# Moving the attention's maxima steps within each run of six score tiles

## The chip, the core and the metric

The kernel runs on one core of a Trainium2 chip. The metric is the device time of one execution in microseconds; the time before is the median of three runs. TensorE (PE) multiplies matrices and writes its results to PSUM, VectorE (DVE), ScalarE (ACT) and GpSimd (POOL) do the rest, SyncE (SP) issues most transfers.

## The reference

One layer of a hybrid block over 2048 latent tokens and 256 context tokens, width 1024, all in fp32. Cut to what matters here:

```python
k_all = jnp.concatenate([k_c, k_x], axis=2)        # 256 context + 2048 latent keys, 2 key heads
v_all = jnp.concatenate([v_c, v_x], axis=2)
s = jnp.einsum('bkgqd,bknd->bkgqn', q, k, preferred_element_type=jnp.float32)
p = jax.nn.softmax(s, axis=-1).astype(v.dtype)     # 8 query heads of 64, 2048 queries
o = jnp.einsum('bkgqn,bknd->bkgqd', p, v)
```

Ahead of it stand a modulated norm and one wide input projection, behind it the merge with a gated branch, an output projection and a squared-ReLU MLP with a residual.

## The kernel before

The program is one straight list of instructions in stages: input projection, attention, merge, MLP. The attention (`attend`) works through 16 units, each a block of 512 queries times a pair of query heads. A unit has 18 key tiles of 128 keys, taken in three runs (groups) of six.

For each key tile, `Unit.scores(j)` takes two PSUM banks (one for each head of the pair) and makes 8 matmuls, four for each head; the two heads use the two halves of the array's rows, so the matmuls run in pairs (line 1780). ScalarE then turns each bank into exponentials (line 1790) and gives it back. The matmuls contract over 64 rows: products of split high and low parts, and one that subtracts the query's reference value, a maximum over its scores.

That maximum is found ahead of time, for later units, by `Unit.maxima(n)`, which does n steps of a list `todo`. A step takes two PSUM banks, makes two matmuls of 512 columns (or four of 256 for the context keys; line 1736) from the high parts alone, and VectorE reduces each bank to a column of maxima (lines 1747 and 1742). A unit has 18 steps: two for the context, 16 for the latent keys. In the first two runs of a unit the steps belong to the next unit (`nxt`), in the third run to the one behind it (`far`); each run does six steps, as long as there is such a unit. When a unit's 18 steps are done, `reference` takes the maximum over them on VectorE (lines 1753 and 1754), and `low_queries` turns the result with four transposes on TensorE (line 186) at the end of the third run.

The values of a run (`Unit.values`, line 1800) are multiplied one run later: `pend` keeps them, and they follow the next run's scores. `values(0)` takes the output's PSUM bank, `leave` copies it out and gives it back (line 1830). Sums of exponentials are built on POOL (line 1823) and for four key tiles on VectorE (line 1820); `join` adds the two, `sums` adds over the partitions on TensorE (line 1842), copied by ScalarE (line 1848).

All score, maxima, transpose and output tiles of the attention share one tag of eight PSUM banks, `self.psum({"b": 8})`. Which bank a tile gets, and so which semaphore its first matmul waits on, is settled when the program is built. The order of work is the order in which `attend` issues it: `fixed` holds TensorE and VectorE to that order, and `order` adds dependencies so that tiles of one tag are first written in the order in which they were made.

Of the kernel before, what the change touches and what calls it, by code (L numbers as in the profile page):

```python
# [70 lines left out]
class Kern:  # L71
# [748 lines left out]
    def attend(self, units, late):  # L820
        begin = self.here()
        pend, self.ready = [], []
        for i, u in enumerate(units):
            at = lambda n: units[n] if 0 <= n < len(units) else None
            nxt, far, old, older = at(i + 1), at(i + 2), at(i - 1), at(i - 2)
            for gi, g in enumerate(range(0, NKT, GROUP)):
                group = range(g, g + GROUP)
                step = nxt if gi < 2 else far
                if not nxt and gi == 0:
                    raws = [self.br_raw(m, self.t2) for m in range(2)]  # L830
                for j in group:
                    u.scores(j)
                    if step:
                        step.maxima(1)
                    if gi == 0 and j == 2 and far:
                        far.load()
                if gi == 2 and nxt:
                    nxt.low_queries()
                if gi == 2 and i in FIRST_INPUTS:
                    next(late, None)  # L840
                for f in pend:
                    f()
                if gi == 1 and far:
                    far.queries()
                if gi == 0 and far:
                    far.cast()
                if gi == 2 and old:
                    old.sums()
                if gi == 0:
                    if older:  # L850
                        older.inverse()
                    if far:
                        far.remainder()
                if gi == 1:
                    if nxt:
                        nxt.reference()
                    if old:
                        old.join()
                if gi == 2 and i in FIRST_INPUTS:
                    next(late, None)  # L860
                if not nxt and gi:
                    self.ready.append(self.br_weights(raws.pop(0), self.t2))
                pend = [lambda u=u, j=j: u.values(j) for j in group]
            pend.append(u.leave)
        for f in pend:
            f()
        units[-2].inverse()
        self.fixed.append(range(begin, self.here()))
# [1039 lines left out]
```

## Time and profile before

| what | us |
|---|---|
| median of three runs (2993.07 to 2994.03) | 2993.59 |
| the profiled execution | 2993.09 |
| its span, first to last instruction | 2991.3 |
| TensorE busy | 2965.5 |
| VectorE busy | 2023.0 |
| ScalarE busy | 1355.5 |

The granted TensorE clock is 0.999 in the mean. The attention's scores run from 757.6 to 1384.1 us of the span. In the rows of a timeline the first number is the start in us from the span's start, the second the length of the merged rows, then engine, line, operation, output and inputs, tile, element types and the count; in brackets stands how long the engine was idle before and what it waited for. In the rows of waits stand the total in us, how often, and the longest.

### The profile page before, as it was taken

What the parts mean: (1) busy time and instruction counts of PE and PEld (TensorE: products, weight loads), DVE (VectorE), ACT (ScalarE), POOL (GpSimd) and SP (SyncE); (2) the same over time, 40 slices, a digit from 0 to 9 for tenths busy, and PEclk for the clock granted to TensorE, in tenths of its full rate; (3) what the DMA queues carried; (4) which work ended last, traced back from release to release, by engine and by line L of the source; (5) the groups of instructions that cost most, each with busy time, mean ns of one, the idle gap of its engine ahead of it and who ended that gap; (6) DMA issues with size and microseconds to landing.
All of it is one profiled execution on the core that took longest, in us unless ns stands there. A gap on an engine that the chain in (4) does not pass through costs nothing.

```text
span 2991.3 us, 39857 instructions
## 1 busy us (share of the span) xinstructions
PE 2965.5 (99%) x14973; PEld 2301.8 (77%) x14973; DVE 2023.0 (68%) x2999; ACT 1355.5 (45%) x2058; POOL 564.9 (19%) x420
## 2 busy tenths in 40 slices
PE   7999999999999999999999999999999999999999
PEld 5888888887656565655888888888888888888887
DVE  6848567585777778886655698786656766654455
ACT  4443434342555555554322264444554344444433
POOL 0000000000788999990000000000000000000000
PEclk9999999999999999999999999999999999999999
DMA  7464646643100000012766558898676544446665
GB/s 240 121 220 122 222 141 196 181 133 109 36 12 16 12 22 20 25 33 97 242 177 183 154 186 314 310 327 305 225 241 227 183 155 155 155 149 219 208 216 204
DMA packets 330275, 485.53 MB, mean 162 GB/s; under 512 B 28953, under 2 KB 161345, under 8 KB 330082
## 3 DMA queue, kind: packets, MB, share of 16 engines
q1 hardware_dynamic: 326242, 478.40, 48.3%
q10 hardware_dynamic: 3840, 4.59, 0.4%
q8 instruction: 117, 1.92, 0.3%
q14 instruction: 76, 0.62, 0.1%
HBM read 348.56 MB, written 134.35 MB: 161 GB/s over the span
## 4 chain that ended last, share of the span: by engine, by line
PE 97%; DVE 2%; DMA 1%; SPq 0%; issue 0%; ACT 0%; ACTq 0%; DVEq 0%
PE b L1362 13%; PE b L1361 13%; PE b L1360 13%; PE b L180 11%; PE b L182 11%; PE b L181 11%; PE b L1780 9%; PE b L1800 8%; PE b L1736 2%; PE b L186 2%; DMA w<-in_w_mod 1%; PE b L1842 0%; PE b L290 0%; DVE ts L1747 0%; DVE ac L1820 0%; DVE f L1490 0%
## 5 line engine op out<-in xcount | busy, mean ns | idle before, releaser
L1467 DVE TENSOR_TENSOR f<-f,f 128x1024 fp32r<-128x1024 f32 x224 | 264.7, 1222 | 257.1 <-ACT f L1466 254.6
L1747 DVE TENSOR_REDUCE ts<-b 128x1 f32<-128x512 f32 x512 | 311.6, 682 | 105.8 <-PE b L1736 105.8
L1360 PE MATMUL b<-f,f 128*128 128x512 f32 x896 | 349.3, 390 | 0.0
L1361 PE MATMUL b<-f,f 128*128 128x512 f32 x896 | 349.0, 390 | 0.0
L1362 PE MATMUL b<-f,f 128*128 128x512 f32 x896 | 348.7, 389 | 0.0
L1466 ACT CAST f<-f 128x1024 fp32r<-128x1024 f32 x224 | 224.6, 1052 | 263.6 <-PE b L1361 255.4
L1780 PE MATMUL b<-t,t 64*128 64x512 f32 x2304 | 330.9, 400 | 0.0
L1780 PEld LDWEIGHTS b<-t,t 64*128 64x128 f32 x2304 | 226.2, 184 | 69.3 <-issue 26.0
L1823 POOL TENSOR_TENSOR ac<-ac,p 128x512 f32<-128x512 f32 x204 | 269.0, 1353 | 43.4 <-ACT p L1790 43.4
L1823 POOL TENSOR_TENSOR ac<-ac,t 128x512 f32<-128x512 f32 x146 | 233.1, 1626 | 0.0
L1790 ACT ACTIVATE p<-b 128x512 f32<-128x512 f32 x384 | 206.7, 598 | 48.3 <-PE b L1780 41.5
L152 DVE TENSOR_TENSOR w<-w,w 128x1024 fp32r<-128x1024 f32 x120 | 146.8, 1223 | 114.4 <-ACT w L148 76.3
L180 PE MATMUL b<-t,w 128*128 128x512 f32 x512 | 203.2, 397 | 0.4 <-DVE ts L1742 0.3
L182 PE MATMUL b<-t,w 128*128 128x512 f32 x512 | 199.7, 390 | 0.0
L181 PE MATMUL b<-t,w 128*128 128x512 f32 x512 | 199.5, 390 | 0.0
L1361 PEld LDWEIGHTS b<-f,f 128*128 128x128 f32 x896 | 168.2, 188 | 35.9 <-DVE f L1467 1.6
L1360 PEld LDWEIGHTS b<-f,f 128*128 128x128 f32 x896 | 168.2, 188 | 34.8
L1362 PEld LDWEIGHTS b<-f,f 128*128 128x128 f32 x896 | 168.2, 188 | 34.8
L180 PE MATMUL b<-w,t 128*128 128x512 f32 (+1 forms) x528 | 191.5, 363 | 0.2 <-DVE t L150 0.2
L148 ACT CAST w<-w 128x1024 fp32r<-128x1024 f32 x120 | 126.0, 1050 | 145.0 <-DMA w<-in_w_in 108.9
L182 PE MATMUL b<-w,t 128*128 128x512 f32 (+1 forms) x528 | 190.5, 361 | 0.1
L181 PE MATMUL b<-w,t 128*128 128x512 f32 (+1 forms) x528 | 190.1, 360 | 0.0
(261 smaller groups left out, 6120.8 us busy)
## 6 DMA issues: line engine op xcount, KB each, us to landing
w<-in_w_in SPq DMA_DIRECT2D x120, 512.0 KB
ao_d<-f SPq DMA_DIRECT2D x224, 256.0 KB
f<-ao_d SPq DMA_DIRECT2D x112, 512.0 KB
f<-w2o_d SPq DMA_DIRECT2D x112, 512.0 KB
f<-in_w_ff SPq DMA_DIRECT2D x48, 1024.0 KB
w2o_d<-f SPq DMA_DIRECT2D x112, 256.0 KB
md<-in_w_mod SPq DMA_DIRECT2D x32, 512.0 KB
f<-x_d SPq DMA_DIRECT2D x64, 256.0 KB
```

Source lines behind the costliest of these rows:

```text
L180: mm(ps, sh, mh, start=start, stop=False, skip_group_check=skip)
L181: mm(ps, sh, ml, start=False, stop=False, skip_group_check=skip)
L182: mm(ps, sl, mh, start=False, stop=stop, skip_group_check=skip)
L1360: mm(ps, wh, hh, start=start and k == 0, stop=False, skip_group_check=True)
L1361: mm(ps, wh, hl, start=False, stop=False, skip_group_check=True)
L1362: mm(ps, wl, hh, start=False, stop=k == len(w) - 1, skip_group_check=True)
L1466: self.nc.scalar.copy(h, f32(l))
L1467: self.nc.vector.tensor_tensor(out=l, in0=f32(l), in1=f32(h), op=ALU.subtract)
L1747: nc.vector.tensor_reduce(out=self.mx[:, t, h, c : c + 1], in_=ps[h], axis=AX.X, op=ALU.max)
L1780: self.nc.tensor.matmul(ps[h], keys[h], q[rows[h]], start=n == 0, stop=n == len(steps) - 1, skip_group_check=True,)
L1800: nc.tensor.matmul(self.o[h * HD : (h + 1) * HD, :], k.V[c][:, i, self.kv * HD : (self.kv + 1) * HD], pt[h], start=j == 0, stop=j == NKT - 1,)
L1823: nc.gpsimd.tensor_tensor(out=self.acc[e][:, h], in0=old[:, h], in1=pt[h], op=ALU.add)
```

## The change

In each run of six key tiles one maxima step followed the scores of each tile. Now none follows the first tile, one follows each of the next four, and two follow the last. Each run still does six steps in the same order.

```diff
                 for j in group:
                     u.scores(j)
-                    if step:
-                        step.maxima(1)
+                    if step and j > g:
+                        step.maxima(1 if j < group[-1] else 2)
                     if gi == 0 and j == 2 and far:
                         far.load()
```

## Prediction

> **What bounds the kernel now.** I read the page first, for the busiest engine and the chain that ends last, and then the timeline of each engine over one stretch of the attention.
>
> ```profile
> span 2991.3 us, 39857 instructions
> PE 2965.5 (99%) x14973; PEld 2301.8 (77%) x14973; DVE 2023.0 (68%) x2999; ACT 1355.5 (45%) x2058; POOL 564.9 (19%) x420
> PE 97%; DVE 2%; DMA 1%; SPq 0%; issue 0%; ACT 0%; ACTq 0%; DVEq 0%
> ```
>
> TensorE (PE) is busy for 99% of the span and carries 97% of the chain that ended last. An edit that neither adds nor removes work can therefore only change how tightly TensorE is packed. The groups of the attention's window give the count of the moved work, and the chain shows what a run of six key tiles costs when no maxima stand in it (the last unit):
>
> ```profile
> L1736 PE MATMUL b<-t,t 64*128 64x512 f32 (+1 forms) x584 | 120.6, 368 | 0.3 <-DVE ts L1747 0.2
> 1356.45 5.68 PE b L1780 x48
> 1367.43 5.71 PE b L1780 x48
> ```
>
> The 584 matmuls are 28 context steps of four and 236 of two: 264 steps, 44 runs of six. One run of TensorE, the third of a unit (L1780 a score set, L1736 a maxima step):
>
> ```profile
> 899.93 1.20 PE L1780 MATMUL b<-t,t 64*128 64x512 f32 x8
> 900.96 0.40 PE L1736 MATMUL b<-t,t 64*128 64x256 f32 x4
> 901.20 1.08 PE L1780 MATMUL b<-t,t 64*128 64x512 f32 x8
> 902.12 0.40 PE L1736 MATMUL b<-t,t 64*128 64x256 f32 x4
> 902.36 1.20 PE L1780 MATMUL b<-t,t 64*128 64x512 f32 x8
> 903.40 0.39 PE L1736 MATMUL b<-t,t 64*128 64x512 f32 x2
> 903.63 1.07 PE L1780 MATMUL b<-t,t 64*128 64x512 f32 x8
> 904.53 0.39 PE L1736 MATMUL b<-t,t 64*128 64x512 f32 x2
> 904.76 1.16 PE L1780 MATMUL b<-t,t 64*128 64x512 f32 x8
> 905.76 0.39 PE L1736 MATMUL b<-t,t 64*128 64x512 f32 x2
> 905.99 1.14 PE L1780 MATMUL b<-t,t 64*128 64x512 f32 x8
> 906.96 0.40 PE L1736 MATMUL b<-t,t 64*128 64x512 f32 x2
> 907.29 0.65 PE L186 MATMUL b<-ident,t 128*128 128x128 f32 x4
> ```
>
> I call the score sets S0 to S5 and read each one's end as the start of the row behind it. A free set takes 0.91 (901.20 to 902.12, 903.63 to 904.53), the first of a run 1.03, a maxima step 0.24, the last step until the next stage 0.33. Nothing waiting, a run would be 1.03 + 5 x 0.91 + 5 x 0.24 + 0.33 = 7.11 us; it is 7.36. So 0.25 is lost to waits, and they have a rhythm: the ends of S1, S3, S5 stand at 902.12, 904.53, 906.96, that is 2.41 and 2.43 apart, where free work of two tiles is 2.30. The waits and ScalarE (ACT), whose exponentials give the score banks back, say why:
>
> ```profile
> PEld b L1780 <- ACT p L1790: 10.9, 50, 0.4
> PEld b L1736 <- DVE ts L1747: 1.6, 5, 0.6
> 901.22 2.19 ACT L1790 ACTIVATE p<-b 128x512 f32<-128x512 f32 x4 [0.55 <-PE b L1780]
> 903.59 2.29 ACT L1790 ACTIVATE p<-b 128x512 f32<-128x512 f32 x4 [0.19 <-PE b L1780]
> 905.96 2.29 ACT L1790 ACTIVATE t<-b 128x512 f32<-128x512 f32 x4
> 915.42 3.25 ACT L1790 ACTIVATE p<-b 128x512 f32<-128x512 f32 x6 [0.66 <-PE b L1780]
> 918.89 1.09 ACT L1790 ACTIVATE p<-b 128x512 f32<-128x512 f32 x2 [0.22 <-PE b L1780]
> 919.98 1.09 ACT L1790 ACTIVATE t<-b 128x512 f32<-128x512 f32 x2
> ```
>
> The weight loads of score sets waited 50 times for an exponential, those of maxima five times for a reduction. There are eight PSUM banks; one holds the unit's output, and each S and each maxima step takes two of the other seven. S2 is the first to need S0's second bank. S0's pair of exponentials starts at 901.22 and takes 1.09 (the rows of two), so ends at 902.31; S2 starts at 902.36 and ends at 903.40, 1.09 behind the exponential's end. So the loop "a score set ends, its two exponentials run, the next but one set may start" turns in 2.41, not 2.30. The Trainium skill, Perfetto Trace Analysis, Optimization Strategy, says that the same gap repeated on the engine that should be full can mean too little PSUM for the next tile. By that rule the trace agrees: 0.25 in each such run.
>
> **The change, part by part.** Per run of six tiles, the first maxima step (0.24 of TensorE, two reductions of VectorE) goes from behind S0 to behind S5's own step. No instruction is added or removed; no DMA is moved: the query load of the next-but-one unit is issued by SP behind the third tile as before. Other stages keep their orders.
>
> *Front of the run.* S1 follows S0 at once: it ends at 1.03 + 0.91 = 1.94 from the run's start instead of 2.19, S2 at 1.94 + 0.24 + 0.91 = 3.09. S0, S1 and the first step fill six banks, S2 takes the seventh and S0's first, the next step takes S0's second and S1's first. S3 then needs S1's second, whoever gets the other freed ones. S0's exponentials start 1.29 into the run (901.22 less 899.93) and ScalarE needs 1.09 a tile, so S1's second ends at 1.29 + 1.09 + 1.09 = 3.47. S3 ends 1.09 later, at 4.56. Without that wait it would end at 3.09 + 0.24 + 0.91 = 4.24. So 0.32 of TensorE's lead is lost at once: before, S3 ended at 4.60 (904.53).
>
> *End of the run.* From S3 to S5 the loop turns once more: 4.56 + 2.41 = 6.97, against 7.03 before (906.96). Behind S5 there are now two steps, 0.24 + 0.33, where one of 0.33 stood: the run ends at 7.54 instead of 7.36. **Price of a third run: +0.18.** In words: S5 is paced by ScalarE through the banks and comes at the same time, 0.06 earlier, and a step that filled the pacing time ahead of it now lies behind it, where nothing waits.
>
> *First run of a unit.* Here ScalarE also has to copy the old sums first and begins later:
>
> ```profile
> 914.18 0.59 ACT L1848 COPY t<-b 128x512 f32<-128x512 f32 x1 [4.94 <-PE b L1842]
> 914.04 1.20 PE L1780 MATMUL b<-t,t 64*128 64x512 f32 x8
> 921.07 0.39 PE L1736 MATMUL b<-t,t 64*128 64x512 f32 x2
> 921.38 3.65 PE L1800 MATMUL b<-p,t 128*64 128x512 f32 x16
> ```
>
> Its exponentials start at 915.42, 1.38 into the run. S1's second ends at 3.56, S3 at 4.65, S5 at 7.06, the run at 7.06 + 0.24 + 0.31 = 7.61, against 7.34 (921.38 less 914.04): **+0.27**.
>
> *Second run of a unit.* The old output's bank is given back at its beginning and the new one is taken behind it, so eight banks turn. S3 waits for S1's second exponential if banks are handed on in the order of the tiles; only one of its two halves then waits. If they go in the order in which they come free, S3 takes one from the first maxima step and does not wait.
>
> ```profile
> 926.69 1.20 PE L1780 MATMUL b<-t,t 64*128 64x512 f32 x8
> 934.21 3.65 PE L1800 MATMUL b<-p,t 128*64 128x512 f32 x16
> 967.30 1.19 PE L1780 MATMUL b<-t,t 64*128 64x512 f32 x8
> 974.53 3.65 PE L1800 MATMUL b<-p,t 128*64 128x512 f32 x16
> ```
>
> These take 7.52 and 7.23; the floor is 7.11. Bounds: -0.12 (7.23 to the floor) and +0.18 (the third run). I take **+0.10**, nearer to the upper, since half the tile is held.
>
> *VectorE (DVE).* The first reduction comes 0.91 later and the last two end about a microsecond later.
>
> ```profile
> 901.40 2.48 DVE L1742 TENSOR_REDUCE ts<-b 128x2 f32<-128x512 f32 x4 [2.11 <-PE b L1736]
> 903.83 4.88 DVE L1747 TENSOR_REDUCE ts<-b 128x1 f32<-128x512 f32 x8
> 915.50 7.29 DVE L1747 TENSOR_REDUCE ts<-b 128x1 f32<-128x512 f32 x12 [5.24 <-PE b L1736]
> 928.14 7.37 DVE L1747 TENSOR_REDUCE ts<-b 128x1 f32<-128x512 f32 x12 [1.97 <-PE b L1736]
> ```
>
> Queued behind them are additions, the query remainder, the reference and the join, and then the next run's reductions. VectorE stood idle for 1.97 to 5.24 before each run's first reduction, and that reduction moves back by 0.91 too, so the delay is absorbed: 0. If the cover were gone, the transposes behind a third run would wait for a bank of a late reduction: a step is 4.88/4 = 1.22 of VectorE, the third run's fourth step is reduced by about 1.94 + 0.43 + 4 x 1.22 = 7.25, before the 7.54 at which they start. Upper bound 0.14 on 14 runs. *POOL and SP:* nothing is moved past either; the sums that POOL adds come from exponentials that start no later at the run's head.
>
> *Unit 0.* Its first two runs are one stretch, as no values stand between, and VectorE paces it: 24 reductions, with a remainder between. The first reduction 0.91 later bounds it at +0.91; the floor is 0, as banks freed late still gate the same last step. I take +0.2, nearer to 0, because most of its steps are gated by TensorE's own order at first.
>
> **Sum.** 14 third runs x 0.18 = 2.5, 14 first x 0.27 = 3.8, 14 second x 0.10 = 1.4, unit 0 0.2: +7.9. The profiled execution took 2993.09 (1.8 around its span), 0.5 under the median of 2993.59. 2993.1 + 7.9 = 3001.0 by that execution, 3001.5 by the median.
>
> **Rivals.** *The order is indifferent (no change, 2993.6).* Exponentials take 6 x 1.09 = 6.54 a run and reductions 7.3, both hidden over run and values together; were the banks enough, each order would run at 7.11 plus the same waits. For it: reductions hardly ever hold TensorE (1.6 in all), and small earlier ends of S5 could cancel the step behind it: at 0.24 earlier instead of 0.06 all is even. Against it: the 2.41 rhythm. The Trainium skill, Perfetto Trace Analysis, Matmuls, asks for groups that rotate through the banks so that draining one overlaps the next group's matmuls; by that rule either order is covered, and the trace agrees only in part, as a run that rotates loses 0.25.
>
> *Faster, by a busier ScalarE.* Before, ScalarE idles within a run (0.19 before 903.59, 0.22 before 918.89). With S0 and S1 together it runs through. If S3 does not have to wait for S1's second exponential, every run falls to the floor: 14 x (7.36 - 7.11) + 14 x (7.34 - 7.11) + 14 x 0.12 = 8.4, so 2985.2. It decides as soon as S3's banks are free by 3.33 - 0.15 = 3.18 of the run instead of 3.47: the 0.29 would need an eighth bank in all runs. I see that in second runs only.
>
> *Slower still.* Second runs pay 0.27 as well, unit 0 its 0.91 and third runs the 0.14 of VectorE: 2.5 + 3.8 + 3.8 + 0.9 + 2.0 = 13.0, 3006.6.
>
> **How the numbers follow.** No change can be told from a difference within 0.2%, 6.0 us. Forecast (2998 to 3004): 0.50; slower still: 0.10; indifferent: 0.28; faster: 0.12. The forecast's lower part (under 2999.6) lies within 0.2%: 0.05 of its 0.50. Hence slower 0.55, same 0.34 (0.28, 0.05, and 0.01 of the faster case, where only second runs gain), faster 0.11. The range leaves out the faster rival and nearly nothing above: 2991 to 3006.5.
>
> **What would show it.** Right: first and third runs of 7.5 to 7.6, S3's first matmul waiting on ScalarE, S5 ending near 7.0, two maxima steps back to back behind it, more waiting of L1780's loads for L1790. Wrong: runs of 7.1 to 7.3, or S3 starting at 3.33; waits of L1736 or L186 for reductions (VectorE after all); a total that moves outside of 757 to 1384 us, where no order changes.

## The result, and the profile after

| | before | after |
|---|---|---|
| median, us (22 runs each) | 2994.1 (2991.99 to 2997.19) | 2999.73 (2997.10 to 3002.41) |
| the profiled execution | 2993.09 | 2999.79 |
| its span | 2991.3 | 2998.0 |
| its attention, first to last score matmul | 626.52 | 632.02 |

The changed kernel is slower by 5.6 us: the ratio is 1.0018, 95% interval 1.0012 to 1.0024. The interval excludes a ratio of 1, so the kernel did get slower, though 5.6 is a little less than the 6.0 (0.2%) that the prediction wanted to see before it spoke of a change. The forecast was +7.9.

The page of the changed kernel's profile shows the same 14973 matmuls and the same bound; TensorE's busy time grew by 4.8 and the span by 6.7. No work was added, so the question is how the matmuls are packed.

```profile
span 2998.0 us, 39869 instructions
PE 2970.3 (99%) x14973; PEld 2293.1 (76%) x14973; DVE 2016.9 (67%) x2999; ACT 1348.8 (45%) x2058; POOL 549.5 (18%) x420
PE 97%; DVE 2%; DMA 1%; issue 0%; ACT 0%; SPq 0%; DVEq 0%; ACTq 0%
```

Where the time went is read from the length of each run, from the start of its first score matmul to the start of the stage behind it. The medians, in us, over the first and second runs of units 1 to 14 and the third runs of units 0 to 13:

| | third runs | first runs | second runs | unit 0's double run | unit 14's third run |
|---|---|---|---|---|---|
| before | 7.363 | 7.354 | 7.261 | 15.60 | 6.35 |
| after | 7.458 | 7.533 | 7.286 | 15.89 | 7.53 |
| difference of the sums | +1.21 | +2.46 | +0.38 | +0.29 | +1.18 |

(The sums are over 14 runs of a kind; unit 14's third run is apart, as no unit needs maxima there any more.) They make +5.5 of attention. The stages between the runs take 279.0 in both. The kernel outside of the attention differs by 1.2, and over all the kernels shown below it lay between 2363.8 and 2367.6, so nothing is read from that.

The third run of the changed kernel on TensorE, at the same place as the one that the prediction shows (start, length, engine, line):

```profile
901.25 2.11 PE L1780 MATMUL b<-t,t 64*128 64x512 f32 x16
...
904.66 1.21 PE L1780 MATMUL b<-t,t 64*128 64x512 f32 x8
905.71 0.40 PE L1736 MATMUL b<-t,t 64*128 64x512 f32 x2
...
907.10 1.20 PE L1780 MATMUL b<-t,t 64*128 64x512 f32 x8
908.14 0.63 PE L1736 MATMUL b<-t,t 64*128 64x512 f32 x4
908.70 0.66 PE L186 MATMUL b<-ident,t 128*128 128x128 f32 x4
```

S0 and S1 are one row of 16. S3 starts at 904.66 and ends at 905.71, 4.46 into the run; S5 ends at 908.14, 6.89; two maxima steps stand behind it, and the transposes begin at 7.45. Both S3 and S5 take 1.04 to 1.05, where a free set takes 0.91. ScalarE in that run, and the waits of the weight loads in the attention (line and what it waited for, total, times, longest):

```profile
902.54 3.10 ACT L1790 ACTIVATE p<-b 128x512 f32<-128x512 f32 x6 [0.55 <-PE b L1780]
905.97 1.08 ACT L1790 ACTIVATE p<-b 128x512 f32<-128x512 f32 x2 [0.33 <-PE b L1780]
```

```profile
PEld b L1780 <- ACT p L1790: 15.2, 48, 1.6
ACT in L148 <- DVE raw L900: 13.6, 4, 8.0
PEld b L186 <- DVE ts L1747: 4.5, 14, 0.4
PEld b L1736 <- DVE ts L1747: 1.0, 4, 0.4
```

Score sets wait longer for exponentials (15.2 us against 10.9), maxima steps no longer than before for reductions (1.0 against 1.6). A first and a second run:

```profile
915.45 2.11 PE L1780 MATMUL b<-t,t 64*128 64x512 f32 x16
...
918.95 1.21 PE L1780 MATMUL b<-t,t 64*128 64x512 f32 x8
920.00 0.40 PE L1736 MATMUL b<-t,t 64*128 64x512 f32 x2
...
922.43 0.64 PE L1736 MATMUL b<-t,t 64*128 64x512 f32 x4
923.00 1.51 PE L1800 MATMUL b<-p,t 128*64 128x512 f32 x6
```

```profile
969.15 2.14 PE L1780 MATMUL b<-t,t 64*128 64x512 f32 x16
...
972.50 1.27 PE L1780 MATMUL b<-t,t 64*128 64x512 f32 x8
...
976.44 1.08 PE L1800 MATMUL b<-p,t 128*64 128x512 f32 x4
```

In the first run S3 ends at 4.55 and S5 at 6.98, and the run at 7.55. In the second run S3 starts at 3.35, where order alone would let it start at 3.33. Only its second half waits, for S1's second exponential, which ends at 972.53 (3.38 into the run). That half stays some 0.2 behind the first: S3's row is 1.27 long, where a free one is 1.08. The lag is carried to the end of the run, at 7.29. Before had nearly the same lag: in the median of 14 second runs the last matmuls of S5's two halves start 0.18 apart before and 0.20 after.

One place was not foreseen. Unit 14's third run, the first one with no maxima, grew by as much as all third runs together. First the changed kernel's timeline there, then before's:

```profile
1347.80 3.28 PE L1780 MATMUL b<-t,t 64*128 64x512 f32 x25
1348.14 1.21 DVE L1835 TENSOR_TENSOR ac<-ac,ac 128x1024 f32<-128x1024 f32 x1
1349.28 1.78 DVE L900 TENSOR_TENSOR raw<-raw,raw 128x512 f32<-128x512 f32 x1
1351.09 0.62 ACT L148 CAST in<-raw 128x512 fp32r<-128x512 f32 x1 [8.04 <-DVE raw L900]
1351.61 4.01 ACT L1790 ACTIVATE p<-b 128x512 f32<-128x512 f32 x8
1352.26 3.14 PE L1780 MATMUL b<-t,t 64*128 64x512 f32 x23 [1.18 <-ACT p L1790]
```

```profile
1343.29 6.42 PE L1780 MATMUL b<-t,t 64*128 64x512 f32 x48
1343.60 1.78 DVE L900 TENSOR_TENSOR raw<-raw,raw 128x512 f32<-128x512 f32 x1
1345.41 0.62 ACT L148 CAST in<-raw 128x512 fp32r<-128x512 f32 x1 [6.56 <-DVE raw L900]
```

Read upward from TensorE's gap of 1.18: it waits for an exponential (L1790); ScalarE's exponentials stand in its queue behind a cast of an input of the merge (L148); the cast waits for VectorE's multiplication of that input (L900), which stands behind the join (L1835) and the late reductions of the unit's second run. The cast starts 3.29 into the run after (1351.09 less 1347.80) and 2.12 before (1345.41 less 1343.29): 1.17 later, which is the run's growth. Not all of that is the moved step: counted from the second run's start the last reduction ends 0.91 later, and the first addition behind it (L1820) takes 2.27 instead of 1.98. In the runs with maxima the next first reduction comes later too, which can take up such a delay. Here there is no next reduction.

### The profile page after: what moved, and what is told of

Its sections match the earlier page's. It is cut to its first block, busy times and chain, and to the rows that moved or that the text cites. A ratio compares the mean times of both kernels' runs of the same rounds, so it can differ in the third digit from the quotient of the medians.

```text
span 2998.0 us, 39869 instructions
## 1 busy us (share of the span) xinstructions
PE 2970.3 (99%) x14973; PEld 2293.1 (76%) x14973; DVE 2016.9 (67%) x2999; ACT 1348.8 (45%) x2058; POOL 549.5 (18%) x420
## 4 chain that ended last, share of the span: by engine, by line
PE 97%; DVE 2%; DMA 1%; issue 0%; ACT 0%; SPq 0%; DVEq 0%; ACTq 0%
PE b L1360 13%; PE b L1361 13%; PE b L1362 13%; PE b L180 11%; PE b L182 11%; PE b L181 11%; PE b L1780 9%; PE b L1800 8%; PE b L1736 2%; PE b L186 2%; DMA w<-in_w_mod 1%; DVE ts L1747 0%; PE b L1842 0%; PE b L290 0%; DMA t<-in_x 0%; DVE f L1490 0%
## 5 line engine op out<-in xcount | busy, mean ns | idle before, releaser
L1780 PE MATMUL b<-t,t 64*128 64x512 f32 x2304 | 321.0, 400 | 1.2 <-ACT p L1790 1.2
L1780 PEld LDWEIGHTS b<-t,t 64*128 64x128 f32 x2304 | 218.6, 184 | 82.1 <-issue 17.1
L1823 POOL TENSOR_TENSOR ac<-ac,p 128x512 f32<-128x512 f32 x204 | 255.8, 1286 | 60.7 <-ACT p L1790 60.7
L1790 ACT ACTIVATE p<-b 128x512 f32<-128x512 f32 x384 | 199.7, 605 | 48.6 <-PE b L1780 43.1
L148 ACT CAST w<-w 128x1024 fp32r<-128x1024 f32 x120 | 126.0, 1050 | 146.4 <-DMA w<-in_w_in 112.8
```

The source lines that it names most:

```text
L1780: self.nc.tensor.matmul(ps[h], keys[h], q[rows[h]], start=n == 0, stop=n == len(steps) - 1, skip_group_check=True,)
L1823: nc.gpsimd.tensor_tensor(out=self.acc[e][:, h], in0=old[:, h], in1=pt[h], op=ALU.add)
```

## The experiments

The theory was the prediction's: the exponentials and the handing on of banks set the pace. The rivals: VectorE's reductions do, or the place of the steps costs by itself, whatever the banks.

**1. Each half of the change alone.** The back half takes the step from ahead of the last tile and puts it behind it:

```diff
-                        step.maxima(1)
+                        step.maxima((1, 1, 1, 1, 0, 2)[j - g])
```

> Steps 1,1,1,1,0,2 behind the six tiles: only the back half of the change. Bank-loop theory (a score set may start when the second exponential of the last but one has ended): followed through with the measured times of one exponential, one reduction and one matmul pair, the runs stay as in the kernel before, about 7.3 (third), 7.4 (first), 7.2 (second); the total is 0 to 2 us above before, with the long wait in unit 14's third run (7.5 instead of 6.3) there again since VectorE ends as late as in the changed kernel. Prediction's reading (every step behind the last tile costs its 0.24): +0.24 in each of 42 runs, +10 us. VectorE theory (late reductions cost): as the changed kernel, +5.5 us.

Measured: 2991.52 us against 2993.62 on the same chip, ratio 0.9991 (0.9982 to 1.0000); attention 625.67, which is 0.85 less than before. The interval reaches no change; the gain is read from the runs of one profile. Third, first and second runs: 7.298, 7.311, 7.239. Unit 14's third run stayed at 6.36, where 7.5 was expected: the last reduction ended 0.72 later than in before, but the addition behind it took 1.25 instead of 1.98, so the cast came at the same time. The same third run:

```profile
899.50 1.20 PE L1780 MATMUL b<-t,t 64*128 64x512 f32 x8
...
904.33 2.08 PE L1780 MATMUL b<-t,t 64*128 64x512 f32 x16
906.25 0.61 PE L1736 MATMUL b<-t,t 64*128 64x512 f32 x4
906.79 0.66 PE L186 MATMUL b<-ident,t 128*128 128x128 f32 x4
```

S5 follows S4 without a wait and ends at 6.75, 0.28 earlier than before. Two steps behind the last tile cost nothing here: the run is shorter by 0.065. The assignment of banks in the built program shows why (M0 to M5 are the maxima steps). Score and maxima tiles take the banks in turn, so with one step fewer ahead of it S5 gets banks that were filled one place earlier: in third and first runs M2's second and S3's first, instead of S3's second and M3's first.

The front half takes the step from behind the first tile and puts it behind the second, one behind the last as before:

```diff
-                        step.maxima(1)
+                        step.maxima((0, 2, 1, 1, 1, 1)[j - g])
```

> Steps 0,2,1,1,1,1: only the front half, the first step goes behind the second tile. Bank-loop theory: two steps in a row need four banks when S1's exponentials have not yet given theirs back, and each later set starts late: runs of 7.7 to 8.0, +20 to +27 us in all. Prediction's reading (nothing more behind the last tile, S5 paced by ScalarE): runs 0.06 shorter than before, -2.5 us. VectorE theory: reductions end nearly as late as in the changed kernel, +5 us.

Measured: 3020.08 us, ratio 1.0088 (1.0074 to 1.0102), +26.5. Third, first and second runs take 8.079, 8.054 and 7.726. TensorE, and what its loads waited for:

```profile
905.31 2.13 PE L1780 MATMUL b<-t,t 64*128 64x512 f32 x16
907.23 0.67 PE L1736 MATMUL b<-t,t 64*128 64x256 f32 x8
907.75 1.68 PE L1780 MATMUL b<-t,t 64*128 64x512 f32 x8
909.05 0.61 PE L1736 MATMUL b<-t,t 64*128 64x512 f32 x2
```

```profile
PEld b L1780 <- ACT p L1790: 14.7, 46, 1.2
PEld b L1736 <- DVE ts L1747: 12.4, 46, 0.4
PEld b L1780 <- DVE ts L1747: 9.1, 39, 0.4
```

S0, S1 and two steps want eight banks, and seven turn: M1 already takes S0's first, and S2 takes S0's second and S1's first. S2 then takes 1.30 (907.75 to 909.05) instead of 0.91, and maxima steps now wait for reductions, 12.4 us where before has 1.6. The halves do not add up (-0.85 and +26.3 in the attention, +5.5 together). The whole change is the front half with one step moved from ahead of S2 to behind S5, and that move takes the price from 26.3 to 5.5. So two score sets together at the head of a run are dear when two steps follow them at once, and much less so when one does. No kernel here takes the step from behind S0 and leaves all others in place, so that place has no measured price of its own.

**2. The inputs of the merge one unit earlier**, so that the cast is not in unit 14's third run, on the changed kernel and on before:

```diff
-FIRST_INPUTS = range(NU - 10, NU - 1)
+FIRST_INPUTS = range(NU - 11, NU - 2)
```

> The changed kernel with the merge's first inputs handled in units 5 to 13 instead of 6 to 14. Theory: the 1.2 us that unit 14's third run lost in the changed kernel is a cast on ScalarE, queued ahead of the exponentials, that waits for a late VectorE multiplication; without it that run takes 5.7 (six tiles without maxima, as in unit 15) instead of 7.5, all other runs stay. Rival (exponentials themselves are late there, or POOL): it stays above 6.5.

> The same move in the kernel before. Theory: unit 14's third run goes from 6.35 to 5.7, other runs unchanged at 7.2 to 7.4; rival: no change of that run.

Measured: 2996.26 and 2993.11 us, one execution each, before 2993.62 beside them. Unit 14's third run took 5.68 in the changed kernel and 5.66 in before. The changed kernel's:

```profile
1347.21 5.75 PE L1780 MATMUL b<-t,t 64*128 64x512 f32 x48
1352.89 0.66 PE L186 MATMUL b<-ident,t 128*128 128x128 f32 x4
```

The gap is gone, the run is as long in both kernels, and the changed kernel's attention falls from 632.02 to 629.72. So the whole 1.18 of the change in this run hangs on the cast's place. Before gains 0.68 in the run and only 0.17 in the attention: its first runs' sum came out 0.5 longer in that execution, for which no cause was found.

**3. Half exponentials**, on the changed kernel and on before: ScalarE reads 256 columns of each score bank.

```diff
-            self.nc.scalar.activation(pt[h], ps[h], AF.Exp)
+            self.nc.scalar.activation(whole[:, h, :H], ps[h][:, :H], AF.Exp)
...
+        twice = whole[:, :, :H].unsqueeze(2).broadcast_to([P, 2, 2, H])
```

> The changed kernel with exponentials of 256 of the 512 queries' columns, each used twice in values and sums (the other half of the softmax is left out). An exponential of 512 takes 0.60 and a ScalarE cast of 1024 takes 1.05, so 256 should take about 0.37 and a tile's pair about 0.7. Bank-loop theory: banks come back early, first and second runs fall to 7.05 to 7.1, third runs to 7.1, up to 7.4 if the transposes behind them then wait for a reduced bank; the difference to the kernel before with the same edit is 0 to 4 us over the runs. Prediction's reading (a step more behind the last tile) and VectorE theory: the difference of the runs stays at 4 us or more, in first runs too (0.17 each).

> The kernel before with the same half exponentials (half of the softmax is left out). Bank-loop theory: all runs fall from 7.2 to 7.4 to the floor of 7.05 to 7.1, about 0.25 x 42 = 10 us less in the attention. If the lost 0.25 is not ScalarE's banks, the runs stay at 7.2 to 7.4.

Measured, one execution each: 2986.31 and 2981.65 us; attention 619.28 and 616.07. The built programs hand their banks on in runs as the two kernels with whole exponentials do, so the order of banks is not what differs. Before's kernel with half exponentials, one group of instructions (min, median and max in ns) and the wait:

```profile
L1790 ACT ACTIVATE p<-b x384: 373/383/447, 759.0 to 1372.2; 128x256 f32<-128x256 f32 x192
```

```profile
PEld b L1780 <- ACT p L1790: 0.2, 1, 0.2
```

With an exponential of 0.38 instead of 0.60 the waits of score sets fall from 10.9 to 0.2, and before's runs to 7.165, 7.146 and 7.038: 0.2 of the quarter of a microsecond by which a run missed its floor was ScalarE's, as the prediction said. The same on the changed kernel makes its first and second runs 7.130 and 7.033: there the cost of the change is gone, wholly. It stays in third runs (7.307 against 7.165) and in unit 14 (7.19 against 5.99), so these have another cause in this setting: VectorE. TensorE's third run with half exponentials in the changed kernel and the waits of its transposes, then the third run in before:

```profile
904.57 0.65 PE L1736 MATMUL b<-t,t 64*128 64x512 f32 x4
905.32 0.66 PE L186 MATMUL b<-ident,t 128*128 128x128 f32 x4
PEld b L186 <- DVE ts L1747: 5.8, 14, 0.4
```

```profile
904.11 0.46 PE L1736 MATMUL b<-t,t 64*128 64x512 f32 x2
904.50 0.66 PE L186 MATMUL b<-ident,t 128*128 128x128 f32 x4
```

From the start of two steps to the transposes it took 0.54 in experiment 1 (906.25 to 906.79); here it takes 0.75. They wait for a bank of a late reduction, the case for which the prediction kept 0.14 a run. With whole exponentials the row of waits is there as well (4.5 us over 14 transposes, above), but S5 comes later, and from the two steps to the transposes it takes 0.56 (908.14 to 908.70), no more than the 0.57 that the sum had.

**4. Half reductions**, on both: VectorE reads 256 columns of each maxima bank.

```diff
-                        out=self.mx[:, t, h, c : c + 1], in_=ps[h], axis=AX.X, op=ALU.max
+                        out=self.mx[:, t, h, c : c + 1], in_=ps[h][:, : TB // 2],
+                        axis=AX.X, op=ALU.max
```

> The changed kernel with reductions over 256 of 512 columns (context steps stay) and exponentials of a thousandth of the score, so that they stay finite without a true maximum (that part of the softmax is changed). Bank-loop theory: first and second runs stay at 7.5 and 7.3, since the late bank is ScalarE's; third runs lose at most the wait of the transposes, 7.36 to 7.46; unit 14's third run falls from 7.5 to 5.7 to 6.4 as VectorE is earlier. VectorE theory: first, second and third runs fall to those of the kernel before, 7.35, 7.25, 7.36.

> The kernel before with the same half reductions and scaled exponentials (that part of the softmax is changed). Bank-loop theory: runs stay at 7.36 (third), 7.35 (first), 7.25 (second); unit 14's third run falls from 6.35 to 5.7 to 6.0. VectorE theory: runs fall toward 7.1.

Measured, one execution each: 2993.27 and 2986.96 us. Unit 0's double run falls to 14.61 and 14.29, where half exponentials left it at 15.26 and 15.04, so VectorE paces it in the main. Unit 14's third run falls to 6.52 and 5.71, as the cast is released earlier. Third runs hardly move (7.434 and 7.388). First runs fall to 7.365 and 7.232, second runs to 7.066 in both kernels. As a test of VectorE's share in first and second runs this failed. The assignment of banks is settled when the program is built, and with shorter reductions it came out otherwise: in before's second runs S3 takes S1's two banks, with half reductions it takes S1's first and M1's first. So the fall in second runs is at least partly a matter of banks, and the two can't be told apart here. Third runs can be read, though: in both kernels S2 and S3 kept their banks there (S3's first half still takes S1's second), and with reductions of half the length these runs changed by +0.03 and -0.02 only. In first runs S1's second bank went to S3's second half instead, and they fell by 0.17 and 0.12. That speaks for the banks and against the reductions: the order in which banks are handed on is a lever of its own.

**5. Banks given out by hand.** Eight tags of one bank each in the attention; a tile takes the banks whose release comes first by an estimate from the traces (exponential 0.6, at a pitch of 0.495; reduction 0.69; score set 0.915).

```diff
+        got = sorted(range(8), key=lambda i: self.rel[i])[:n]
...
-        ps = [k.bank([TB]) for _ in range(2)]
+        got = k.plan.take(2)
+        ps = [k.plan.tile(i, [TB]) for i in got]
+        k.plan.read(got, "act", 0.915, 0.495, 0.6, 0.25)
```

On the changed kernel and on before:

> The changed kernel with banks given by hand in the order in which they come free. Bank-loop theory: 7.24 (third), 7.36 (first), 7.10 (second) instead of 7.46, 7.53, 7.29: about 8 us less than the changed kernel, and second runs cost nothing over the kernel before. Rival (the step behind the last tile): runs stay.

> The kernel before with banks given by hand in the order in which they come free. Bank-loop theory: 7.16 to 7.2 (third), 7.28 (first), 7.10 (second) instead of 7.36, 7.35, 7.26; unit 14's third run stays at 6.35. Rival: runs stay.

Measured, one execution each: 2993.55 and 2988.64 us, before 2993.92 beside them; attention 625.71 and 622.81. Third, first and second runs are 7.323, 7.382 and 7.153 in the changed order, 7.261, 7.325 and 7.145 in the old one. The waits of score sets (their line has moved, L1819 for L1780, L1829 for L1790), changed order first:

```profile
PEld b L1819 <- ACT p L1829: 5.1, 17, 1.7
```

```profile
PEld b L1819 <- ACT p L1829: 1.6, 6, 0.5
```

Third runs came out 0.06 to 0.08 longer than expected. The changed kernel gains 6.3 us of attention from its banks alone, before 3.7. Of the 4.3 us that the change cost in its runs with the built order (+1.2, +2.5, +0.4, +0.29), 1.7 is left (about 0.75 in third and in first runs each, 0 in second runs, 0.2 in unit 0). The other 1.2 stays in unit 14's third run (7.65 against 6.46), where it is the cast. So most of the change's price in the runs is not in the order as such, but in that order with these banks, as far as one execution of each shows.

**6. Toward a faster kernel.** The back half with the early inputs (the two diffs of 1 and 2 together on before), and both with the banks given out by hand:

> Steps 1,1,1,1,0,2 (the back half alone) with the merge's first inputs in units 5 to 13. Bank-loop theory: runs as in the back-only kernel, 7.30 (third), 7.31 (first), 7.24 (second), unit 14's third run 5.7 instead of 6.36: 2 to 3 us under the kernel before. Rival (a step behind the last tile costs 0.24): above before.

> As the last one, and the attention's tiles are given their banks by hand, always the bank that by the measured times comes free first; the second half of a score set then waits for the exponential and the first half takes a reduced bank. Bank-loop theory: runs of 7.16 to 7.2 (third), 7.28 (first), 7.05 (second), unit 14's third run 5.7, in all about 6 us under the kernel before. If banks are not what holds TensorE: runs as in the back-only kernel.

Measured: without the banks 2991.58 us, ratio 0.9990 (0.9981 to 1.0000); with them 2988.57, ratio 0.9983 (0.9974 to 0.9992), 5.35 faster than before beside it. It is faster than either kernel. Its attention takes 621.33, 5.2 less than before. The waits, and a second run:

```profile
PEld b L1819 <- ACT p L1829: 0.6, 2, 0.3
```

```profile
925.93 1.21 PE L1819 MATMUL b<-t,t 64*128 64x512 f32 x8
...
933.05 1.51 PE L1843 MATMUL b<-p,t 128*64 128x512 f32 x6
```

That run takes 7.12; third and first runs are 7.198 and 7.327 in the median. Only unit 0's double run is longer, 16.19 against 15.60. The banks alone had given 2988.64 in one execution, with 622.81 of attention, so most of the gain is theirs; what the other two edits add to them, 1.5 of attention in single executions, was not measured by itself.

## Why the prediction was right, and where it was not

**The bound and the rhythm: right.** A run is paced by "a score set ends, its two exponentials run, the next but one set may start". Half exponentials took the waits away and brought the runs down by 0.2; in the changed kernel S3 to S5 is 6.89 - 4.46 = 2.43, where the prediction had 2.41. The Trainium skill, Perfetto Trace Analysis, Optimization Strategy, reads a repeated gap on the busiest engine as a possible lack of PSUM: by that rule experiment 5 agrees in part, as the same eight banks, given out in another order, took away about a third of the gap (3.7 us of attention, where half exponentials took 10.4).

**Third runs, +0.18: mis-sized, +0.09 measured (+1.2 for 2.5).** The failed step is "ScalarE needs 1.09 a tile", which put S3's end at 4.56. With S0 and S1 both ready ScalarE does not stop, and six exponentials took 3.10: 0.60 for the first and 0.50 for each behind it, 1.00 a tile. S3 ended at 4.46, S5 at 6.89. The price of 1.09 came from pairs that each began behind a wait. The Trainium skill, ScalarE: Activation LUTs, What ACT_TABLE_LOAD costs, says that ACTIVATEs back to back overlap by about 93 ns; by that rule the trace agrees: an exponential takes 0.60 and in a row starts 0.50 behind the last, an overlap of about 0.10.

**First runs, +0.27: mis-sized, +0.18 measured (+2.5 for 3.8),** for the same reason: S3 ended at 4.55 instead of 4.65, S5 at 6.98 instead of 7.06.

**Second runs, +0.10: mis-sized, +0.03 (+0.4 for 1.4).** S3 does take S1's two banks, in the order of the tiles, the case that the prediction gave the higher price, and only one of its halves waits, as it said. What failed is the price: before already carried a lag of 0.18 between the halves to the end of these runs, and the change made it 0.20.

**Unit 0, +0.2: +0.29,** and paced in the main by VectorE, as half reductions showed.

**VectorE "absorbed: 0": wrong in one place, for +1.18** (0.3 of it an addition that took longer). The reason given, that the next run's first reduction moves back too, does not hold for the run that has no reductions. What follows there on VectorE was named (the query remainder, the reference, the join), but not L900, nor that ScalarE's queue holds a cast for it ahead of exponentials. The trace of before shows that cast waiting 6.56 us, and unit 14's run at 6.35 where other runs without maxima take 5.7. It was there to be read.

**"A step that filled the pacing time ahead of it now lies behind it": wrong as a general sentence.** For the changed order the arithmetic held, as S5 there takes S3's second bank. But the same move by itself (experiment 1) shortens the runs, since S5 then takes banks that come free earlier. What a step costs hangs on the banks that it moves, not on its place behind the last tile.

So two errors lay in opposite directions: the runs cost 4.3 for a foreseen 7.9, and unit 14's 1.2 was not foreseen. That part of the agreement is luck: without unit 14 the median would have been near 2998.5, at the lower end of the forecast's 2998 to 3004. *The rivals:* "indifferent" fails on the waits of score sets and on the interval. "Faster" named the right reason to doubt, a ScalarE that runs through, but S3 did not get its banks at 3.18 in third and first runs. "Slower still" fails on second and third runs. Of the signs against the forecast one came: the transposes (L186) wait for reductions, 4.5 us in all. It had no price in the whole kernel: the last step and the transposes stand 0.32 apart in both kernels, and before they waited as long for exponentials at the same place, as its row shows:

```profile
PEld b L186 <- ACT t L1790: 5.1, 14, 0.4
```

The others did not: first and third runs are not at 7.1 to 7.3, S3 does not start at 3.33 in them, and L1736's waits for reductions did not grow.

## What to carry to other kernels

Where a buffer passes from tile to tile in a fixed order, a step that is moved changes which buffer each later tile gets; work out the table of who takes whose buffer before pricing the move, and consider giving buffers out by their expected release. Price a producer at its pitch in a row where the move lets it run through, not at its pitch behind waits. Look at the last iterations by themselves: there the cover that absorbs a delay everywhere else can be missing, and one waiting instruction in an in-order queue holds all behind it.

## What was unexpected in the hardware

Two single VectorE instructions took several times as long as others of their group. In the kernel with the back half alone, and in the one with the back half and the early inputs:

```profile
1110.40 6.92 DVE L1820 TENSOR_TENSOR ac<-ac,p 128x1024 f32<-128x1024 f32 x1
```

```profile
1312.01 6.33 DVE L900 TENSOR_TENSOR raw<-raw,raw 128x512 f32<-128x512 f32 x1
```

The group of the first has a mean of 1.94, that of the second a median of 0.68. The first runs in which they stand took 8.51 and 11.14 instead of 7.31. The second kernel's profiled execution, at 2994.85, lay 3.3 above the median of its runs, about the 3.8 that its one run was too long. POOL was adding sums through most of both, until 1116.23 and 1317.80 by its rough spans, and they ended 1.09 and 0.54 behind that, about as long as the shortest of their groups take (1.21 and 0.68). The Trainium skill, GPSIMD Engine Reference, Specifications, says that GpSimd shares its SBUF interfaces with VectorE and contends with its instructions of two SBUF inputs, which both of these are. POOL adds sums through most of the attention, though, and no other instruction of those groups was held so long, so the cause stays open.
